# Four orders of the long and short passes in the up projection of a gated hybrid block

## The chip, the cores and the metric

The kernel runs on one core of one Trainium2 chip. The metric is the device time of the whole program in microseconds (us), the median of several runs. The kernel before took 1475.83 us (3 runs, 1475.67 to 1475.99).

## What is computed

The reference is one block on a sequence of 256 rows of 2048 features: an RMS norm, an input projection, three kinds of attention, a gated merge with an output projection, and a feed-forward part. The change lies in the feed-forward part alone:

```
h2 = rms_norm(x, g_ffn[l])
u = causal_depthwise_conv(h2 @ w_up[l], conv_w[l], conv_b[l])
u_gate, u_val = jnp.split(u, 2, axis=-1)
x = x + (jax.nn.silu(u_gate) * u_val) @ w_down[l]
```

`w_up` is 2048 x 11264 (twice D_FF = 5632), all in float32. The change is in the product `h2 @ w_up`.

## The kernel before, in words

A float32 product is made of passes in a rounded type (fp32r). Each operand is split into a high part and the low rest: the high part is the operand rounded to fp32r, the low part is what the rounding left. High by high, low by high and high by low are summed in PSUM, in float32.

**The stages.** In order of time they are the memory's keys and values, the input projection with the three attentions (line tags mq, f, s, g), the gated merge (g, b), the output projection (o), the up projection (u) with its convolution, and the down projection (d). Products other than u run through `passes` (lines 148 to 154) or `three` (lines 284 to 288) with three matmuls of up to 512 columns, each with a weight load of its own.

**The up stage.** The tile hT holds h2 transposed: for each of the 16 k tiles (128 features each, KT = 16) 512 columns, 256 of the high part and then 256 of the low part. The stage walks over 11 blocks of four feature tiles (f0 = 0, 4, ..., 40) and in each over the two halves of w_up (s = 0 for the gate, s = 1 for the value). One f0 with one s is called a *round* here; there are 22. A round fills four PSUM banks, ps[0] to ps[3], one for each tile of 128 features. It takes eight pieces of w_up of 128 x 1024 (two k tiles by 512 features). `piece` (lines 135 to 146) loads a piece by a DMA on SyncE's queue into raw, ScalarE casts it into hi (line 141), and VectorE subtracts to get lo (line 142). There are four buffers each of raw, hi and lo.

For each k tile and each of the four feature tiles there are two matmuls, with w_up as the stationary operand:
- the **long pass** (line 1152): weights hi, moving all 512 columns of hT(k), so it gives high by high and high by low at once, into the whole bank;
- the **short pass** (line 1153): weights lo, moving only the first 256 columns (the high part), added to the first half of the same bank.

So a k tile is eight matmuls, a round 128, and the stage 1408 long and 1408 short ones, each with a load of 128 x 128 weights (LDWEIGHTS). Before, they stand as long 0, short 0, long 1, short 1 and so on: always alternating, with the two passes of one feature tile side by side.

**What stands around them.** After each piece, `tick()` moves pending generators on by a step, at most two at a time: the convolutions of the round before (`conv`, from line 1113, which copy the upper half of a bank out at line 1118, add the lower half at 1120, scale, apply three taps and a bias, and for s = 1 form the product that goes into aT), and in the background sums of w_down that the down stage uses later (`weight_sums`). In the first rounds some transposes of the last parts of hT (line 195) stand between the passes. No order is pinned by hand for the matmuls of this stage; the framework schedules them in the order in which the code issues them, and places the other engines' work beside them.

Of the kernel before, what the change touches and what calls it, by code (L numbers as in the profile page):

```python
# [16 lines left out]
S = 256  # L17
# [18 lines left out]
BLOCKS = 14  # L36
WINDOW = 2
GS = 3


@with_exitstack
def hybrid_block(
# [25 lines left out]
    nc = tc.nc  # L68
# [12 lines left out]
    def bank(name):  # L81
        return pp.tile([P, 512], F32, tag="bank", name=name)
# [14 lines left out]
    def later(gen):  # L97
        waiting.append(gen)
# [3 lines left out]
    def tick(beside=True):  # L102
        if beside:
            for g in background:
                next(g, None)
        while waiting and len(active) < WINDOW:
            active.append([waiting.popleft(), 0])
        for a in list(active):
            if a[1] > 0:
                a[1] -= 1  # L110
                continue
            try:
                a[1] = next(a[0]) or 0
            except StopIteration:
                active.remove(a)
# [19 lines left out]
    def piece(src, a, n, name):  # L135
        raw = wp.tile([P, PIECE], F32, tag="raw", name=f"raw_{name}")
        hi = wp.tile([P, PIECE], F32R, tag="hi", bufs=SBUFS, name=f"hi_{name}")
        lo = wp.tile([P, PIECE], F32R, tag="lo", bufs=SBUFS, name=f"lo_{name}")
        m = a * n
        pin(nc.sync.dma_start(raw[:, :m].rearrange("p (a n) -> p a n", a=a), src))  # L140
        pin(nc.scalar.copy(hi[:, :m], raw[:, :m]))  # L141
        pin(nc.vector.tensor_tensor(lo[:, :m], raw[:, :m], hi[:, :m].bitcast(F32), ALU.subtract))  # L142
        return (
            hi[:, :m].rearrange("p (a n) -> p a n", a=a),
            lo[:, :m].rearrange("p (a n) -> p a n", a=a),
        )
# [9 lines left out]
    def product(x_of, w, nk, n0, n, name):  # L156

        ps = [bank(f"{name}_{t}") for t in range(NT)]
        wv = w.rearrange("(k p) n -> p k n", p=P)
        for k in range(0, nk, 2):  # L160
            a = min(2, nk - k)
            wh, wl = piece(wv[:, k : k + a, n0 : n0 + n], a, n, f"{name}_{k}")
            order = [(j, t) for j in range(a) for t in range(NT)]
            if k + a == nk:
                order.sort(key=lambda jt: jt[1])
            for j, t in order:
                xk = x_of(k + j)
                xs_ = xk[:, t * P : (t + 1) * P], xk[:, S + t * P : S + (t + 1) * P]
                three(ps[t][:, :n], *xs_, (wh[:, j], wl[:, j]), k + j == 0, k + j == nk - 1)
            tick()  # L170
        return ps
# [30 lines left out]
    def k_tiles(name):  # L202

        most = xt_pool.tile([P, KT - 2, 2 * S], F32R, tag="xt", name=name)
        rest = []

        def at(k):
            if k < KT - 2:
                return most[:, k]
            if not rest:  # L210
                rest.append(xt_pool.tile([P, 2, 2 * S], F32R, tag="xu", name=f"{name}_rest"))
            return rest[0][:, k - KT + 2]

        at.pair = lambda p: most[:, 2 * p : 2 * p + 2]
        return at
# [74 lines left out]
    def pair_sums(pair, w, groups):  # L290

        v = pair.bitcast(F32).rearrange("p k (l c) -> p k l c", l=2)
        a, r = (half.rearrange("p (i q) -> p i q", i=4) for half in (w[:, :512], w[:, 512:]))
        nc.vector.tensor_tensor(w[:, :512].rearrange("p (k c) -> p k c", k=2), v[:, :, 0], v[:, :, 1], ALU.add)

        a10 = a[:, 1:2].to_broadcast([P, 2, P])
        nc.vector.tensor_tensor(r[:, FS3 : FS1 + 1], a[:, 0:4:3], a10, ALU.subtract)
        nc.vector.scalar_tensor_tensor(r[:, FS2], r[:, FS1], -1.0, a[:, 0], ALU.mult, ALU.subtract)
        nc.vector.tensor_tensor(r[:, FS4], r[:, FS2], a[:, 2], ALU.add)
        for dst, which in groups:  # L300
            nc.scalar.copy(dst[..., 0, :], r[:, which])
        for dst, which in groups:
            nc.vector.tensor_tensor(dst[..., 1, :], r[:, which], dst[..., 0, :].bitcast(F32), ALU.subtract)
# [261 lines left out]
    def block(name, dt=F32):  # L565
        return bp.tile([P, 1024], dt, tag="blk", name=name)
# [105 lines left out]
    for k in range(KT):  # L672
# [18 lines left out]
        for _ in range(0 if k < 3 else 1 if k < 8 else 3):  # L691
            if squares:
                j, t = squares.popleft()
# [36 lines left out]
    ps = proj(C_MQ, MEM_W, "mq")  # L730
# [36 lines left out]
    for c in range(3):  # L767
        ps = proj(c * 512, 512, f"f{c}")
# [7 lines left out]
    ps = proj(1536, 512, "f3")  # L776
# [3 lines left out]
    ps = proj(2048, 262, "f4")  # L780
# [58 lines left out]

    xs = cst.tile([P, GS, 4, 2, P], F32R, tag="xres", name="xs")  # L840

    def x_sums():
        for p in range(GS):
            pair_sums(xT.pair(p), block(f"xw_{p}"), [(xs[:, p], slice(0, 4))])
            yield 2
# [9 lines left out]
    for c in range(3):  # L855
        ps = proj(C_SB + c * 512, 512, f"s{c}")
# [51 lines left out]
    ps = proj(C_SB + 1536, 512, "s3")  # L908
# [4 lines left out]
    ps = proj(C_SB + 2048, 256, "s4")  # L913
# [39 lines left out]
    for m in range(2):  # L953
        gate = []
        for b, plan in enumerate(g_plans[m]):
# [40 lines left out]
            if not plan:  # L996
                biases()
                for n in range(2):
                    ps = proj(c0 + n * 512, 512, f"g{n}_{b}")
# [12 lines left out]
        for n in range(2):  # L1012
            acc = gate[branches[0][3]][n]
            for i, (w, k0, nk, b) in enumerate(branches):
                ps = product(lambda k: oT[:, k0 + k], w[0], nk, (2 * m + n) * 512, 512, f"b{2 * m + n}_{b}")
# [15 lines left out]
    hT = k_tiles("hT")  # L1031
# [34 lines left out]
    for nb, plan in enumerate(o_plans):  # L1066
# [4 lines left out]
        for n in range(2):  # L1071
            for t in range(NT):
                o = xres[:, t, nb * PIECE + n * 512 : nb * PIECE + (n + 1) * 512]
# [12 lines left out]
    for i in range(2):  # L1086
        background.append(
            weight_sums(
                lambda name, i=i: ff.tile([P, 1024], F32, tag=f"end{i}", bufs=1, name=name), 8, 6, delay=14 + 2 * i
# [23 lines left out]
    def conv(ps, f, s):  # L1113
        if not pads:
            padded()
        ct = s * FT + f
        cr = cp.tile([P, S], F32, tag="cr", bufs=2, name=f"cr_{f}_{s}")
        nc.scalar.copy(cr, ps[:, S:])
        u = pads[f % 2]
        nc.vector.tensor_tensor(cr, cr, ps[:, :S], ALU.add)  # L1120
        nc.vector.tensor_tensor(u[:, 2:], cr, rbc, ALU.mult)  # L1121
        y = cp.tile([P, S], F32, tag="y", bufs=6, name=f"y_{f}_{s}")
        tap = lambda j: taps[:, j, ct : ct + 1]
        nc.scalar.activation(y, u[:, 2:], AF.Identity, scale=tap(2), bias=tap(3))  # L1124
        nc.vector.scalar_tensor_tensor(y, u[:, 1 : S + 1], tap(1), y, ALU.mult, ALU.add)
        nc.vector.scalar_tensor_tensor(y, u[:, 0:S], tap(0), y, ALU.mult, ALU.add)
        if s == 0:
            nc.scalar.activation(y, y, AF.Silu)
            ys[f] = y
        else:  # L1130
            g = ys.pop(f)
            nc.vector.tensor_tensor(g, g, y, ALU.mult)
            split_to(a_pair(f // 2)[:, f % 2], g)
        return
        yield

    for f0 in range(0, FT, 4):
        if f0 == FA:
            assert not halves
            for g in background:  # L1140
                deque(g, 0)
            background.clear()
        for s in range(2):
            ps = [bank(f"u{f0 + i}_{s}") for i in range(4)]
            c0 = s * D_FF + f0 * P
            for k in range(0, KT, 2):
                hi, lo = piece(upv[:, k : k + 2, c0 : c0 + 512], 2, 512, f"u{f0}_{s}_{k}")
                for j in range(2):
                    first, last = k + j == 0, k + j == KT - 1
                    for i in range(4):  # L1150
                        c = slice(i * P, (i + 1) * P)
                        nc.tensor.matmul(ps[i], lhsT=hi[:, j, c], rhs=hT(k + j), start=first, stop=False)  # L1152
                        nc.tensor.matmul(  # L1153
                            ps[i][:, :S], lhsT=lo[:, j, c], rhs=hT(k + j)[:, :S], start=False, stop=last
                        )
                tick()
            for i in range(4):
                later(conv(ps[i], f0 + i, s))
# [41 lines left out]
    for nb, plan in enumerate(d_plans):  # L1200
# [5 lines left out]
        for t in range(NT):  # L1206
            for n in range(2):
                c = nb * PIECE + n * 512
                o = xres[:, t, c : c + 512]
                nc.vector.tensor_tensor(o, o, X[t][n], ALU.add)  # L1210
                if (nb, t, n) == (1, 1, 1):
                    nc.scalar.dma_start(ov[:, t, c : c + 256], o[:, :256])
                    c, o = c + 256, o[:, 256:]
# [35 lines left out]
```

## Time and profile before

| | |
|---|---|
| median of 3 runs | 1475.83 us |
| the profiled execution's own time | 1476.04 us |
| its span in the trace | 1474.3 us |
| TensorE busy | 1468.7 us, 7337 matmuls |
| VectorE busy | 1195.8 us (81%) |
| ScalarE busy | 840.3 us (57%) |
| GpSimd busy | 20.4 us (1%) |
| DMA | 369.42 MB, 251 GB/s on average |
| up stage | from 746.7 us to about 1245.8 us |

In the rows of groups, the columns are the line, the engine, the operation, the tiles written and read, the shape (partitions x elements), the count, the busy time in us and the mean duration of one in ns, and last the idle time of the engine just before them. In a time line each row begins with the start in us from the span's start and the duration in us. A matmul's recorded duration runs past the start of the next one, since matmuls are pipelined; the distance from start to start is what one of them takes of TensorE's time. In rows of windows, the columns are the stretch, its length, the busy time and count of each engine (PE, PEld, DVE, ACT, POOL), the granted TensorE clock, the DMA share and GB/s.

### The profile page before, as it was taken

To read this page: it belongs to the slowest core of one execution; us is meant where nothing else is said; L and a number is where in the kernel's file an instruction comes from. 1 tells how busy PE (TensorE), PEld (TensorE's weight loads), DVE (VectorE), ACT (ScalarE), POOL (GpSimd) and SP (SyncE) were. 2 spreads that over 40 slices of the span, in tenths; PEclk is the share of its full clock that TensorE was granted. 3 is DMA by queue.
4 is the path that set the end of the run, shared out by engine and by line. 5 is a ranking of instruction groups with operands and counts; after the bars stand their busy time and mean duration, and the time that the engine had idled before them with its cause. 6 is when DMAs were issued, how large, how long until landed. Compare 5 with 4: busy or idle time off the path is not lost.

```text
span 1474.3 us, 20665 instructions
## 1 busy us (share of the span) xinstructions
PE 1468.7 (100%) x7337; PEld 1239.0 (84%) x7337; DVE 1195.8 (81%) x1818; ACT 840.3 (57%) x1194; POOL 20.4 (1%) x46
## 2 busy tenths in 40 slices
PE   9999999999999999999999999999999999999998
PEld 7888888888888888888888888888888888888887
DVE  5777676777588899997788888888888877997877
ACT  6755454464364555546666656656556555674664
POOL 0000000021000000000000000000000000000000
PEclk9999999999999999999999999999999999999999
DMA  9686787687768576878768888888888866798796
GB/s 313 198 274 194 219 285 216 179 277 219 247 203 272 168 222 207 279 250 282 238 207 272 279 283 285 272 271 287 279 279 283 260 185 199 241 315 276 257 328 224
DMA packets 205526, 369.42 MB, mean 251 GB/s; under 512 B 13530, under 2 KB 82030, under 8 KB 205166
## 3 DMA queue, kind: packets, MB, share of 16 engines
q1 hardware_dynamic: 204094, 365.99, 77.7%
q10 hardware_dynamic: 1328, 2.11, 0.4%
q8 instruction: 57, 0.93, 0.2%
q14 instruction: 47, 0.39, 0.1%
HBM read 335.54 MB, written 32.51 MB: 250 GB/s over the span
## 4 chain that ended last, share of the span: by engine, by line
PE 98%; DMA 0%; DVE 0%; ACT 0%; SPq 0%; POOL 0%; issue 0%; POOLq 0%; DVEq 0%
PE u L1152 22%; PE u L1153 11%; PE xd L288 4%; PE xd L287 4%; PE xd L286 4%; PE xg L288 3%; PE xg L287 3%; PE xg L286 3%; PE f L288 2%; PE f L286 2%; PE f L287 2%; PE s L286 2%; PE s L288 2%; PE s L287 2%; PE g L286 2%; PE g L288 2%
## 5 line engine op out<-in xcount | busy, mean ns | idle before, releaser
L1152 PE MATMUL u<-hT,hi_u 128*128 128x512 f32 x1232 | 436.2, 399 | 0.0
L1153 PE MATMUL u<-hT,lo_u 128*128 128x256 f32 x1232 | 345.9, 281 | 0.0
L1152 PEld LDWEIGHTS u<-hT,hi_u 128*128 128x128 f32 x1232 | 231.5, 188 | 57.5
L142 DVE TENSOR_TENSOR lo_u<-raw_u,hi_u 128x1024 fp32r<-128x1024 f32 x176 | 215.0, 1222 | 71.1 <-ACT hi_u L141 69.0
L141 ACT CAST hi_u<-raw_u 128x1024 fp32r<-128x1024 f32 x176 | 184.7, 1050 | 150.5 <-PE u L1152 134.1
L1153 PEld LDWEIGHTS u<-hT,lo_u 128*128 128x128 f32 x1232 | 232.7, 189 | 0.0
L281 DVE TENSOR_TENSOR lo_d<-raw_d,hi_d 128x1024 fp32r<-128x1024 f32 x88 | 106.6, 1221 | 20.8 <-ACT hi_d L280 18.0
L280 ACT CAST hi_d<-raw_d 128x1024 fp32r<-128x1024 f32 x88 | 91.8, 1053 | 48.1 <-PE xd L287 22.3
L280 ACT CAST hi_g<-raw_g 128x1024 fp32r<-128x1024 f32 (+1 forms) x64 | 61.7, 972 | 38.4 <-PE xg L287 10.2
L281 DVE TENSOR_TENSOR lo_g<-raw_g,hi_g 128x1024 fp32r<-128x1024 f32 (+1 forms) x64 | 70.9, 1117 | 4.3 <-ACT hi_g L280 4.3
L141 ACT CAST hi_f<-raw_f 128x1024 fp32r<-128x1024 f32 (+1 forms) x40 | 38.6, 967 | 52.0 <-PE f L287 47.3
L142 DVE TENSOR_TENSOR lo_f<-raw_f,hi_f 128x1024 fp32r<-128x1024 f32 (+1 forms) x40 | 44.7, 1119 | 27.9 <-ACT hi_f L141 26.0
L286 PE MATMUL xd<-hi_d,aT 128*128 128x512 f32 x170 | 66.2, 389 | 0.0
L287 PE MATMUL xd<-hi_d,aT 128*128 128x512 f32 x170 | 66.2, 389 | 0.0
L288 PE MATMUL xd<-lo_d,aT 128*128 128x512 f32 x170 | 66.2, 389 | 0.0
L142 DVE TENSOR_TENSOR lo_s<-raw_s,hi_s 128x1024 fp32r<-128x1024 f32 (+1 forms) x40 | 44.7, 1116 | 24.3 <-ACT hi_s L141 23.4
L141 ACT CAST hi_s<-raw_s 128x1024 fp32r<-128x1024 f32 (+1 forms) x40 | 38.4, 961 | 43.9 <-PE s L287 28.3
L1152 PE MATMUL u<-hT_rest,hi_u 128*128 128x512 f32 x176 | 63.1, 398 | 0.0
L141 ACT CAST hi_b<-raw_b 128x1024 fp32r<-128x1024 f32 x32 | 33.7, 1053 | 43.2 <-PE b L287 21.5
L142 DVE TENSOR_TENSOR lo_g<-raw_g,hi_g 128x1024 fp32r<-128x1024 f32 x32 | 39.3, 1232 | 22.7 <-ACT hi_g L141 22.3
L1124 ACT ACTIVATE y<-u,taps 128x256 f32<-128x256 f32 x88 | 49.2, 595 | 13.0 <-DVE u L1121 13.0
L141 ACT CAST hi_g<-raw_g 128x1024 fp32r<-128x1024 f32 x32 | 33.6, 1051 | 37.4 <-PE g L287 35.1
(481 smaller groups left out, 3531.9 us busy)
## 6 DMA issues: line engine op xcount, KB each, us to landing
raw_u<-in_w_up_dram SPq DMA_DIRECT2D x176, 512.0 KB, 4.9
raw_g<-in_w_in_dram SPq DMA_DIRECT2D x96, 512.0 KB, 4.3
raw_d<-in_w_down_dram SPq DMA_DIRECT2D x66, 512.0 KB, 5.5
pre_d<-in_w_down_dram SPq DMA_DIRECT2D x88, 256.0 KB, 4.6
kept_d<-pre_d SPq DMA_DIRECT2D x44, 512.0 KB, 6.3
raw_f<-in_w_in_dram SPq DMA_DIRECT2D x32, 512.0 KB, 4.8
raw_s<-in_w_in_dram SPq DMA_DIRECT2D x32, 512.0 KB, 3.9
raw_o<-in_w_out_dram SPq DMA_DIRECT2D x25, 512.0 KB, 5.6
```

The lines of the kernel that those rows point to most:

```text
L141: pin(nc.scalar.copy(hi[:, :m], raw[:, :m]))
L142: pin(nc.vector.tensor_tensor(lo[:, :m], raw[:, :m], hi[:, :m].bitcast(F32), ALU.subtract))
L280: nc.scalar.copy(hi[:, :n], src)
L281: nc.vector.tensor_tensor(lo[:, :n], src, hi[:, :n].bitcast(F32), ALU.subtract)
L286: fix(nc.tensor.matmul(o, lhsT=ah, rhs=w[0], start=first, stop=False))
L287: fix(nc.tensor.matmul(o, lhsT=al, rhs=w[0], start=False, stop=False))
L288: fix(nc.tensor.matmul(o, lhsT=ah, rhs=w[1], start=False, stop=last))
L1124: nc.scalar.activation(y, u[:, 2:], AF.Identity, scale=tap(2), bias=tap(3))
L1152: nc.tensor.matmul(ps[i], lhsT=hi[:, j, c], rhs=hT(k + j), start=first, stop=False)
L1153: nc.tensor.matmul(ps[i][:, :S], lhsT=lo[:, j, c], rhs=hT(k + j)[:, :S], start=False, stop=last)
```

## The change

The eight passes of a k tile are taken in one of four orders, and the orders change from round to round. In the strings, h is a long pass, l a short one, and the digit is the feature tile. Every bank still gets its long pass ahead of its short one in each k tile. The matmuls themselves, their operands and their number stay.

```diff
+UP_ORDERS = [
+    [(int(o[i + 1]), o[i]) for i in range(0, 16, 2)]
+    for o in ("h0l0h1l1h2l2h3l3", "h0h1l0h2l1h3l2l3", "h0h1l0l1h2h3l2l3", "h0h1h2h3l0l1l2l3")
+]
...
                 for j in range(2):
                     first, last = k + j == 0, k + j == KT - 1
-                    for i in range(4):
+                    for i, part in UP_ORDERS[(f0 // 2 + s) % len(UP_ORDERS)]:
                         c = slice(i * P, (i + 1) * P)
-                        nc.tensor.matmul(ps[i], lhsT=hi[:, j, c], rhs=hT(k + j), start=first, stop=False)
-                        nc.tensor.matmul(
-                            ps[i][:, :S], lhsT=lo[:, j, c], rhs=hT(k + j)[:, :S], start=False, stop=last
-                        )
+                        if part == "h":
+                            nc.tensor.matmul(ps[i], lhsT=hi[:, j, c], rhs=hT(k + j), start=first, stop=False)
+                        else:
+                            nc.tensor.matmul(
+                                ps[i][:, :S], lhsT=lo[:, j, c], rhs=hT(k + j)[:, :S], start=False, stop=last
+                            )
```

The orders are counted from 0. Blocks with f0 = 0, 8, 16, 24, 32, 40 take order 0 for the gate and order 1 for the value; blocks with f0 = 4, 12, 20, 28, 36 take orders 2 and 3. In the changed kernel the long pass is line 1157, the short one line 1159, and other lines below the table stand four or more further down.

TensorE, the round f0 = 4, s = 0 (order 2), the first k tile of its second piece, before. The names are the bank, hT, and the piece's hi or lo:

```order
L1152 MATMUL u_0_7183<-hT,hi_u_0_2_7239 128x512
L1153 MATMUL u_0_7183<-hT,lo_u_0_2_7240 128x256
L1152 MATMUL u_0_7184<-hT,hi_u_0_2_7239 128x512
L1153 MATMUL u_0_7184<-hT,lo_u_0_2_7240 128x256
L1152 MATMUL u_0_7185<-hT,hi_u_0_2_7239 128x512
L1153 MATMUL u_0_7185<-hT,lo_u_0_2_7240 128x256
L1152 MATMUL u_0_7186<-hT,hi_u_0_2_7239 128x512
L1153 MATMUL u_0_7186<-hT,lo_u_0_2_7240 128x256
```

The same k tile in the changed kernel:

```order
L1157 MATMUL u_0_7183<-hT,hi_u_0_2_7239 128x512
L1157 MATMUL u_0_7184<-hT,hi_u_0_2_7239 128x512
L1159 MATMUL u_0_7183<-hT,lo_u_0_2_7240 128x256
L1159 MATMUL u_0_7184<-hT,lo_u_0_2_7240 128x256
L1157 MATMUL u_0_7185<-hT,hi_u_0_2_7239 128x512
L1157 MATMUL u_0_7186<-hT,hi_u_0_2_7239 128x512
L1159 MATMUL u_0_7185<-hT,lo_u_0_2_7240 128x256
L1159 MATMUL u_0_7186<-hT,lo_u_0_2_7240 128x256
```

Two successions of long behind long and two of short behind short have come in where all had alternated.

TensorE, the next round (f0 = 4, s = 1, order 3) at the same place, in the changed kernel (before, it alternates like the piece above):

```order
L1157 MATMUL u_1_7422<-hT,hi_u_1_2_7474 128x512
L1157 MATMUL u_1_7423<-hT,hi_u_1_2_7474 128x512
L1157 MATMUL u_1_7424<-hT,hi_u_1_2_7474 128x512
L1157 MATMUL u_1_7425<-hT,hi_u_1_2_7474 128x512
L1159 MATMUL u_1_7422<-hT,lo_u_1_2_7475 128x256
L1159 MATMUL u_1_7423<-hT,lo_u_1_2_7475 128x256
L1159 MATMUL u_1_7424<-hT,lo_u_1_2_7475 128x256
L1159 MATMUL u_1_7425<-hT,lo_u_1_2_7475 128x256
```

All four long passes now stand ahead of the four short ones.

VectorE, in the round after that one (f0 = 8, s = 0, order 0), before. lo_u_0_4 and lo_u_0_6 are the splits of the third and fourth piece, cr and u the convolution's tiles:

```order
L142 TENSOR_TENSOR lo_u_0_4_7754<-raw_u_0_4_7752,hi_u_0_4_7753 128x1024
L1120 TENSOR_TENSOR cr_1_7686<-cr_1_7686,u_1_7422 128x256
L1120 TENSOR_TENSOR cr_1_7697<-cr_1_7697,u_1_7423 128x256
L1121 TENSOR_TENSOR u_6983<-cr_1_7686,rbc 128x256
L1121 TENSOR_TENSOR u_6985<-cr_1_7697,rbc 128x256
L142 TENSOR_TENSOR lo_u_0_6_7776<-raw_u_0_6_7774,hi_u_0_6_7775 128x1024
```

And in the changed kernel:

```order
L146 TENSOR_TENSOR lo_u_0_4_7754<-raw_u_0_4_7752,hi_u_0_4_7753 128x1024
L146 TENSOR_TENSOR lo_u_0_6_7776<-raw_u_0_6_7774,hi_u_0_6_7775 128x1024
L1124 TENSOR_TENSOR cr_1_7686<-cr_1_7686,u_1_7422 128x256
L1124 TENSOR_TENSOR cr_1_7697<-cr_1_7697,u_1_7423 128x256
L1125 TENSOR_TENSOR u_6983<-cr_1_7686,rbc 128x256
L1125 TENSOR_TENSOR u_6985<-cr_1_7697,rbc 128x256
L146 TENSOR_TENSOR lo_u_0_8_7798<-raw_u_0_8_7796,hi_u_0_8_7797 128x1024
```

The split of the fourth piece has moved ahead of the convolution's first four steps, and the later splits of the round have moved up likewise. SyncE's and GpSimd's rows stand as before.

## The prediction

> **What bounds the kernel now.** I read the page first: the span, its engine rows and its costliest groups. It is one execution on one core.
>
> ```profile
> span 1474.3 us, 20665 instructions
> PE 1468.7 (100%) x7337; PEld 1239.0 (84%) x7337; DVE 1195.8 (81%) x1818; ACT 840.3 (57%) x1194; POOL 20.4 (1%) x46
> L1152 PE MATMUL u<-hT,hi_u 128*128 128x512 f32 x1232 | 436.2, 399 | 0.0
> L1153 PE MATMUL u<-hT,lo_u 128*128 128x256 f32 x1232 | 345.9, 281 | 0.0
> L142 DVE TENSOR_TENSOR lo_u<-raw_u,hi_u 128x1024 fp32r<-128x1024 f32 x176 | 215.0, 1222 | 71.1 <-ACT hi_u L141 69.0
> ```
>
> TensorE is busy all the time, and the two lines that the change reorders never waited (0.0 in the last column; the fifth row is the split that makes lo). The durations of 399 and 281 ns are no price: matmuls are pipelined and these overlap. What an order can change is the distance from one matmul's start to the next, and the time line has the starts. Next come the whole stage by the windows, and what stands around line L1152 and around the casts that feed it:
>
> ```profile
> 746.00:1246.00 500.00, 500.00 (x2839) 434.01 (x2838) 420.58 (x723) 294.55 (x452) 0.00 (x0) 1.00 0.82 261
> ```
>
> ```profile
> L1152 PEld LDWEIGHTS u<-hT,hi_u x1232: 187/188/190, 746.5 to 1242.5; 128*128 128x128 f32 x176
> L1152 PE MATMUL u<-hT,hi_u x1232: 389/398/476, 746.7 to 1242.6; 128*128 128x512 f32 x176
> L1152 PE MATMUL u<-hT_rest,hi_u x176: 392/398/403, 768.0 to 1245.5; 128*128 128x512 f32 x176
> ```
>
> ```profile
>   PE u L1152: 134.1, 112
> ```
>
> The stage lasts 500 us; TensorE is busy in all of it at a granted clock of 1.00, VectorE in 420.58, ScalarE in 294.55, and DMA takes a 0.82 share. The last row is from the casts' own waits (line L141): ScalarE sat idle 134.1 us, 112 times, until a long pass had freed a buffer of hi. The producers are ahead of TensorE. So the stage is 1408 long and 1408 short passes back to back: from the first long pass at 746.7 to the last at 1245.5 there are 1407 pairs in 498.8 us, 354.5 ns each, with a few transposes among them. A short pass and a long one make a pair.
>
> **What one pair costs.** This is the time line of TensorE in the present order, three pairs:
>
> ```profile
> 905.22 0.40 PE L1152 MATMUL u<-hT_rest,hi_u 128*128 128x512 f32 x1
> 905.45 0.28 PE L1153 MATMUL u<-hT_rest,lo_u 128*128 128x256 f32 x1
> 905.57 0.40 PE L1152 MATMUL u<-hT_rest,hi_u 128*128 128x512 f32 x1
> 905.81 0.28 PE L1153 MATMUL u<-hT_rest,lo_u 128*128 128x256 f32 x1
> 905.93 0.40 PE L1152 MATMUL u<-hT_rest,hi_u 128*128 128x512 f32 x1
> 906.17 0.28 PE L1153 MATMUL u<-hT_rest,lo_u 128*128 128x256 f32 x1
> 906.28 0.40 PE L1152 MATMUL u<-hT_rest,hi_u 128*128 128x512 f32 x1
> ```
>
> From 905.22 to 906.28 are 1.06 us for three pairs: **353 ns a pair**, about 236 from a long pass to the short one and 117 back. The three are not equal (0.35, 0.36, 0.35); this cycle repeats through the stage. The new orders put long behind long and short behind short, which the stage does not have. Other stages do, each matmul with weights of its own as here: long ones in the down stage, then passes of 256 columns (line tags s, 300 to 307 us; the rows left out are seven more of the same).
>
> ```profile
> 1299.65 0.39 PE L286 MATMUL xd<-hi_d,aT 128*128 128x512 f32 x1
> 1299.87 0.39 PE L287 MATMUL xd<-hi_d,aT 128*128 128x512 f32 x1
> 1300.10 0.39 PE L288 MATMUL xd<-lo_d,aT 128*128 128x512 f32 x1
> 1300.33 0.39 PE L286 MATMUL xd<-hi_d,aT 128*128 128x512 f32 x1
> ```
>
> ```profile
> 302.81 0.28 PE L286 MATMUL s<-hi_s,xT 128*128 128x256 f32 x1
> ...
> 303.77 0.28 PE L288 MATMUL s<-lo_s,xT 128*128 128x256 f32 x1
> ```
>
> Three steps of 0.68 us in all give 227 ns for long behind long; eight steps of 0.96 us give 120 for short behind short. Together 347: **6 ns less than the present pair**. That alternation need not cost the 6 ns shows in this stage itself. After the transposes at 752 us the same alternating order runs for 16 us in another cycle; the first and last long pass of 20 pairs there:
>
> ```profile
> 761.03 0.39 PE L1152 MATMUL u<-hT,hi_u 128*128 128x512 f32 x1
> ...
> 767.97 0.39 PE L1152 MATMUL u<-hT_rest,hi_u 128*128 128x512 f32 x1
> ```
>
> 6.94 us by 20 is 347 ns. So TensorE has a settled pace of 347 per pair and a worse cycle of 353, and before is in the worse one nearly throughout. Which one it falls into hangs on what preceded, by a few ns.
>
> **The change, part by part.** Nothing is added or taken away: 1408 long and 1408 short passes, the same loads, the same DMAs. SyncE's and GpSimd's order is untouched.
> - Rounds. The index is (f0/2 + s) mod 4 with f0 in steps of 4: even blocks take orders 0 and 1, odd blocks 2 and 3. Eleven blocks give 6, 6, 5 and 5 rounds. Order 0 is the present one. In order 1 one of eight successions in a k tile is long-long and one short-short, in order 2 two and two, in order 3 three and three; the rest alternate, the seam between k tiles included (each order ends short and begins long). A round has 16 k tiles, so 16 x (6x1 + 5x2 + 5x3) = 496 times a long-short and a short-long succession are replaced by a long-long and a short-short.
> - Price of one replacement: 227 + 120 - 353 = -6 ns (-6.6 with the three pairs taken as 353.3 and the three steps as 226.7). 496 x 6.6 = **3.3 us less**, if the successions that still alternate stay at 353.
> - VectorE and ScalarE. After an order-3 round the list puts some splits one place earlier, ahead of the convolution's taps. They cost nothing while TensorE waits for neither: VectorE has 500 - 420.58 = 79 us free in the stage, and a stage 3.3 us shorter leaves 76. If that cover were gone, one split late would hold TensorE by at most its own length, which the row of line L142 gives as 1222 ns; I take zero, since not one wait of TensorE for it is on record there.
> - Buffers. In order 3 the last long pass on a hi tile comes three short passes (0.36 us) earlier, so casts may start earlier; lo is first needed later in the k tile. Both only loosen. New accumulators are asked for together at a round's start in order 3; each bank was filled two rounds (some 45 us) before, and its copying out is queued behind that round's end, so zero here as well.
>
> What no row shows is a succession such as long-long-short-short repeating. From below: every pair of the 16 changed rounds at 347, that is 16 x 64 = 1024 pairs x 6.6 = 6.8 us less. If the order-0 rounds that follow a changed round come into the good cycle as well (5 x 64 pairs), another 2.1. From above: the longs behind the last short of the stage:
>
> ```profile
> 1245.71 0.28 PE L1153 MATMUL u<-hT_rest,lo_u 128*128 128x256 f32 x1
> 1245.83 0.40 PE L286 MATMUL xd<-hi_d,aT 128*128 128x512 f32 x1
> ...
> 1246.78 0.39 PE L287 MATMUL xd<-hi_d,aT 128*128 128x512 f32 x1
> ```
>
> The row at 1246.78 is the fourth long behind the first: 0.95 us for four, 237 each, 11 above the settled 227, so a long pass is slower for a while after short ones. Four such longs and four shorts at 120 make a k tile of 1.427 us against 4 x 0.3533 = 1.413: +14 ns. In all 256 changed k tiles that is 3.5 us more. The opposite seam is milder: behind passes of 262 columns three longs take 0.69 us, 230 each.
>
> ```profile
> 192.45 0.40 PE L286 MATMUL s<-hi_s,xT 128*128 128x512 f32 x1
> ...
> 193.14 0.40 PE L286 MATMUL s<-hi_s,xT 128*128 128x512 f32 x1
> ```
>
> And the first shorts behind longs are not dearer than 120: three steps take 0.35 us.
>
> ```profile
> 293.81 0.28 PE L286 MATMUL s<-hi_s,xT 128*128 128x256 f32 x1
> ...
> 294.16 0.28 PE L286 MATMUL s<-hi_s,xT 128*128 128x256 f32 x1
> ```
>
> With four longs at 230 and four shorts at 118 a k tile takes 1.39 us, 21 ns less; I lean to this side and take the 3.3 us, nearer to the middle of the ends than to either.
>
> **The sum.** The profiled execution took 1476.04 us (span 1474.3 and 1.7 around it). Less 3.3 is 1472.7. The median of the runs shown, 1475.83, lies 0.2 lower, so I predict **1472.5 us**.
>
> **The rivals.**
> - *All settles.* The changed rounds find the 347 pace throughout: 1475.83 - 6.8 = 1469.0, down to 1467 with the order-0 rounds. For it: 347 is what all settled rows give, in this stage too. Against: the present order leaves that pace and stays at 353 for hundreds of us.
> - *Order does not matter.* Each pass costs the same wherever it stands, 353 a pair being this stage's own price (its tiles, its banks, the traffic beside it): 1475.8, give or take 1. For it: TensorE's clock is already 1.00 and nothing waits. Against: 347 at 761 us, with the same tiles. The Trainium skill, in "TensorE: Matmul & The Clock Gate", section "Back-to-back issue gap", gives 518 cycles for 512 columns and 262 for 256, whatever the neighbour; at its 2.4 GHz I estimate 325 ns a pair from that page in any order, hence no change. The trace does not agree with the figure (353), and by the two cycles not with the independence either.
> - *Shorts unsettle the longs behind them* (slower). The 237 ns at 1246 us is paid in every run of longs, as no run of longs is longer than four: +3.5 us, 1479.3. It decides once a changed pair is above 353.3; above 356.2 (2.95 us by 1024 pairs) it would show as slower by 0.2%. For it: that seam comes out of this very order. Against: the 230 at 192 us.
> - A short pass too brief to cover a load of weights would be worse (the load's record is 188 ns), but in the rows at 303 us every short pass has such a load and they stand 120 apart; I leave it no chance of its own.
>
> **How the numbers follow.** My forecast 36 in 100, with a range of its own from 1471 to 1474.3; all settles 21; order does not matter 18; shorts unsettle 25. 0.2% is 2.95 us, about what a measurement of this kernel can tell from no change: below 1472.88 is faster. The forecast is cut in two by it, 18 and 18; all settles is faster; the third is within; of the slower case 15 are beyond 1478.78 and 10 within. So faster 0.39, same 0.46, slower 0.15. The range 1468.0 to 1479.3 takes the bounds of both unknown sides; left out are the good cycle in order-0 rounds too, and a slower case beyond its price.
>
> **What would show it.** In the time line of the changed kernel: pairs of order 0 at 353 or 347; in orders 1 to 3 a k tile of eight passes between 1.387 and 1.427 us, order 3 below order 2 below order 1 if my count of replacements is right; about equal at 1.387 if all settles; 1.413 in every order if order does not matter; long-long steps near 237 if shorts unsettle. TensorE must keep 0.0 idle on both lines. A wait on hi, lo or a bank there, or a k tile outside those bounds, makes the prediction wrong in its premise, not in its size.

## The result, and the profile after

The changed kernel takes 1471.12 us (median of 10 runs, 1470.69 to 1473.0), the kernel before 1475.91 us beside it: a ratio of 0.9969, 95% interval 0.9959 to 0.9979, or 4.8 us less. One of the ten executions of the kernel before took 2846.36 us and is not in the ratio; its other nine lie between 1475.46 and 1477.38. The profiled span went from 1474.3 to 1469.3 us. The page of the changed kernel, its span, TensorE's row and its two lines:

```profile
span 1469.3 us, 20673 instructions
PE 1464.2 (100%) x7337; PEld 1238.8 (84%) x7337; DVE 1192.3 (81%) x1818; ACT 837.7 (57%) x1194; POOL 20.3 (1%) x46
L1157 PE MATMUL u<-hT,hi_u 128*128 128x512 f32 x1232 | 393.5, 395 | 0.0
L1159 PE MATMUL u<-hT,lo_u 128*128 128x256 f32 x1232 | 274.2, 280 | 0.0
```

As many matmuls as before, and 0.0 of waiting on both lines. The casts still wait for TensorE to free a buffer, 121.0 us in 96 waits, as the waits of line L145 (before, L141) show:

```profile
  PE u L1157: 121.0, 96
```

So the stage is bound as it was, and TensorE itself goes through the same matmuls faster. Where, the starts of the rounds tell. These are the first long passes of the second to the seventh round in the time line of the changed kernel:

```profile
770.65 0.48 PE L1157 MATMUL u<-hT,hi_u 128*128 128x512 f32 x1
...
793.32 0.40 PE L1157 MATMUL u<-hT,hi_u 128*128 128x512 f32 x1
...
815.62 0.40 PE L1157 MATMUL u<-hT,hi_u 128*128 128x512 f32 x1
...
838.05 0.40 PE L1157 MATMUL u<-hT,hi_u 128*128 128x512 f32 x1
...
860.25 0.39 PE L1157 MATMUL u<-hT,hi_u 128*128 128x512 f32 x1
...
882.84 0.40 PE L1157 MATMUL u<-hT,hi_u 128*128 128x512 f32 x1
```

The distances are 22.67 us for the round of order 1, 22.30 for order 2, 22.43 for order 3, **22.20 for order 0**, and 22.59 for order 1 again. This sequence repeats to the end of the stage (22.59, 22.30, 22.44, 22.19 us by the trace's nanoseconds). Before, a round took 22.61 us, except the first of all, which has the transposes in it, and the second (22.69). The stage has become 4.7 us shorter:

| order | rounds that changed | us a round, before and after | us in all |
|---|---|---|---|
| 0 | 5 (behind order 3) | 22.61, 22.19 | 2.1 |
| 1 | 6 | 22.61, 22.59 (the first: 22.69, 22.67) | 0.1 |
| 2 | 5 | 22.61, 22.30 | 1.6 |
| 3 | 5 | 22.61, 22.44 | 0.9 |

The largest part came in the rounds in which **no matmul has moved**. There the passes alternate at the good pace, which before showed for some 16 us only; first and last long pass of 20 pairs in the changed kernel:

```profile
849.85 0.39 PE L1157 MATMUL u<-hT,hi_u 128*128 128x512 f32 x1
...
856.78 0.39 PE L1157 MATMUL u<-hT,hi_u 128*128 128x512 f32 x1
```

6.93 us by 20 is 347 ns. In the kernel before, the pace changes at two places, and at both transposes stand between the passes, whose own order stays the same. At the first the stage comes into the good pace, across 16 transposes:

```profile
749.88 0.40 PE L1152 MATMUL u<-hT,hi_u 128*128 128x512 f32 x1
...
752.00 0.40 PE L1152 MATMUL u<-hT,hi_u 128*128 128x512 f32 x1
...
752.35 1.91 PE L195 MATMUL hT<-ident,xres_again 128*128 128x128 f32 x16
...
754.79 0.39 PE L1152 MATMUL u<-hT,hi_u 128*128 128x512 f32 x1
...
756.18 0.39 PE L1152 MATMUL u<-hT,hi_u 128*128 128x512 f32 x1
```

Six pairs take 2.12 us ahead of them, 353 ns each, and four take 1.39 behind, some 347 each. At the second, between the first and the second round, it falls out of it across two:

```profile
770.74 0.38 PE L1048 MATMUL rp<-ident,rb 128*128 128x128 f32 x2
770.88 0.48 PE L1152 MATMUL u<-hT,hi_u 128*128 128x512 f32 x1
771.19 0.28 PE L1153 MATMUL u<-hT,lo_u 128*128 128x256 f32 x1
771.31 0.40 PE L1152 MATMUL u<-hT,hi_u 128*128 128x512 f32 x1
...
773.43 0.40 PE L1152 MATMUL u<-hT,hi_u 128*128 128x512 f32 x1
```

From 771.31 on six pairs take 2.12 us again. The first long pass behind the two transposes holds TensorE for 0.31 us, which is why the second round took 22.69. No run here leaves these two transposes out.

In a k tile of order 1 (in the time line, equal neighbours are one row with their count, so x2 are two passes):

```profile
875.77 0.63 PE L1157 MATMUL u<-hT,hi_u 128*128 128x512 f32 x2
876.24 0.28 PE L1159 MATMUL u<-hT,lo_u 128*128 128x256 f32 x1
876.35 0.40 PE L1157 MATMUL u<-hT,hi_u 128*128 128x512 f32 x1
876.59 0.28 PE L1159 MATMUL u<-hT,lo_u 128*128 128x256 f32 x1
876.70 0.40 PE L1157 MATMUL u<-hT,hi_u 128*128 128x512 f32 x1
876.94 0.40 PE L1159 MATMUL u<-hT,lo_u 128*128 128x256 f32 x2
877.18 0.63 PE L1157 MATMUL u<-hT,hi_u 128*128 128x512 f32 x2
```

The tile runs from 875.77 to 877.18, 1.41 us, no shorter than the old order's (4 x 0.3533 = 1.413). Its two longs together take 0.47 us, where settled ones took 0.454. Order 2, eight passes from the middle of one k tile to the middle of the next, and the start of the following half:

```profile
894.69 0.63 PE L1157 MATMUL u<-hT,hi_u 128*128 128x512 f32 x2
895.15 0.39 PE L1159 MATMUL u<-hT,lo_u 128*128 128x256 f32 x2
895.38 0.63 PE L1157 MATMUL u<-hT,hi_u 128*128 128x512 f32 x2
895.85 0.40 PE L1159 MATMUL u<-hT,lo_u 128*128 128x256 f32 x2
896.08 0.63 PE L1157 MATMUL u<-hT,hi_u 128*128 128x512 f32 x2
```

1.39 us. The rows are rounded to 0.01 us and cannot tell the lengths of the two halves apart (697 and 696 ns from start to start by the trace's nanoseconds), but the halves are not alike inside: the row of shorts lasts 0.39 in the first and 0.40 in the second. In the first the starts of the two shorts and of the next long stand 117 and 112 ns apart, in the second 114 and 119. That small difference turns out to matter below.

### The profile page after: what moved, and what is told of

Its sections match the earlier page's. It is cut to its first block, busy times and chain, and to the rows that moved or that the text cites. A ratio compares the mean times of both kernels' runs of the same rounds, so it can differ in the third digit from the quotient of the medians.

```text
span 1469.3 us, 20673 instructions
## 1 busy us (share of the span) xinstructions
PE 1464.2 (100%) x7337; PEld 1238.8 (84%) x7337; DVE 1192.3 (81%) x1818; ACT 837.7 (57%) x1194; POOL 20.3 (1%) x46
## 4 chain that ended last, share of the span: by engine, by line
PE 99%; DVE 0%; ACT 0%; POOL 0%; issue 0%; POOLq 0%; DVEq 0%
PE u L1157 22%; PE u L1159 11%; PE xd L292 4%; PE xd L291 4%; PE xd L290 4%; PE xg L292 3%; PE xg L290 3%; PE xg L291 3%; PE f L290 2%; PE f L292 2%; PE f L291 2%; PE s L290 2%; PE s L292 2%; PE s L291 2%; PE g L290 2%; PE b L292 2%
## 5 line engine op out<-in xcount | busy, mean ns | idle before, releaser
L1157 PE MATMUL u<-hT,hi_u 128*128 128x512 f32 x1232 | 393.5, 395 | 0.0
L1159 PE MATMUL u<-hT,lo_u 128*128 128x256 f32 x1232 | 274.2, 280 | 0.0
L145 ACT CAST hi_u<-raw_u 128x1024 fp32r<-128x1024 f32 x176 | 184.9, 1051 | 151.8 <-PE u L1157 121.0
L1159 PEld LDWEIGHTS u<-hT,lo_u 128*128 128x128 f32 x1232 | 222.3, 188 | 26.7
L1157 PEld LDWEIGHTS u<-hT,hi_u 128*128 128x128 f32 x1232 | 210.8, 188 | 27.6
L285 DVE TENSOR_TENSOR lo_d<-raw_d,hi_d 128x1024 fp32r<-128x1024 f32 x88 | 106.7, 1222 | 20.6 <-ACT hi_d L284 17.6
L145 ACT CAST hi_f<-raw_f 128x1024 fp32r<-128x1024 f32 (+1 forms) x40 | 38.6, 967 | 52.2 <-PE f L291 47.3
L145 ACT CAST hi_s<-raw_s 128x1024 fp32r<-128x1024 f32 (+1 forms) x40 | 38.4, 961 | 43.9 <-PE s L291 27.4
L145 ACT CAST hi_b<-raw_b 128x1024 fp32r<-128x1024 f32 x32 | 33.5, 1051 | 41.7 <-PE b L291 18.7
L1157 PE MATMUL u<-hT_rest,hi_u 128*128 128x512 f32 x176 | 56.4, 395 | 0.0
L145 ACT CAST hi_g<-raw_g 128x1024 fp32r<-128x1024 f32 x32 | 33.6, 1051 | 38.3 <-PE g L291 34.7
```

Of the source, the lines that this page charges most:

```text
L285: nc.vector.tensor_tensor(lo[:, :n], src, hi[:, :n].bitcast(F32), ALU.subtract)
L1159: nc.tensor.matmul(ps[i][:, :S], lhsT=lo[:, j, c], rhs=hT(k + j)[:, :S], start=False, stop=last)
```

## Experiments

Two explanations stood against each other at first. The *count theory* is the prediction's own sum: each long-long with a short-short in place of two alternating successions saves 6.6 ns, and what still alternates stays as it was. The *path theory*: for a given order TensorE falls into one of several lasting cycles, and what preceded decides which. The order-0 rounds of the changed kernel speak for the second; the runs were to say whether that lasts and what decides. Edits are against the changed kernel; they replace the index of the table, unless the text says otherwise. In them f0 // 2 + s is the round and k + j the k tile, both counted from 0. Ratios are to the kernel before.

**Order 3 in one round.**

```diff
-for i, part in UP_ORDERS[(f0 // 2 + s) % len(UP_ORDERS)]:
+for i, part in UP_ORDERS[3 if f0 // 2 + s == 1 else 0]:
```

> Order 3 in the second round alone (f0 = 0, s = 1), order 0 in the other 21. Path theory (the pace of alternating passes hangs on what preceded it, and lasts): the 20 rounds behind it take 22.19 us each, as the order-0 rounds behind order 3 did in the changed kernel, against 22.61 before: 20 x 0.42 = 8.4 us less, and 0.2 in the second round, so about 1467.3 us. Count theory (each long-long and short-short in place of two alternating successions saves 6.6 ns, order-0 rounds stay at 22.61): 48 replacements, 0.3 us less, 1475.6 us. If the good pace lasts for one round only: 0.6 us less, 1475.3.

1475.87 us, ratio 1.0000 (0.9991 to 1.0009). The order-0 rounds behind it take 22.61 us each. The path theory's forecast failed in its simple form: order 3 ahead is not enough. The count theory's 1475.6 is met here within the noise.

**Order 3 in one k tile.**

```diff
+for i, part in UP_ORDERS[3 if (f0 // 2 + s, k + j) == (1, 4) else 0]:
```

> Order 3 in a single k tile (the fifth of the second round), order 0 everywhere else: eight matmuls in another order out of 2816. Path theory: if one run of four longs and four shorts is enough to change the cycle, all that follows runs at 22.19 us a round, 20.7 rounds x 0.42 = 8.7 us less, 1467.2 us; if it takes more than one such tile, 1475.9. Count theory: three replacements, 0.02 us, 1475.9.

1476.19 us, ratio 1.0003 (0.9994 to 1.0012). The tile itself took 1.388 us, the next one 1.411, and all behind it stayed in the worse cycle.

**A tour of the orders.**

```diff
+for i, part in UP_ORDERS[int("0100200300100200301000"[f0 // 2 + s])]:
```

> Orders by round 0 1 0 0 2 0 0 3 0 0 1 0 0 2 0 0 3 0 1 0 0 0: order 0 behind each of the others, for up to three rounds, and each of the others behind good and behind bad rounds. Path theory: order-0 rounds come in two prices, 22.19 and 22.61 us, set by the order that stood last before them (behind order 3: 22.19), the rounds of one group all alike. Count theory: every order-0 round at 22.61, order 1 at 22.50, order 2 at 22.40, order 3 at 22.29, and 208 replacements x 6.6 = 1.4 us less in all, 1474.5.

A single execution: 1468.55 us, span 1466.8. The reading rests on the rounds in its trace. All of the 14 order-0 rounds behind the second round take 22.19 us, whether behind order 1, 2 or 3, and for up to three rounds on end; order 1 is at 22.59, order 2 at 22.29, order 3 at 22.44. The count theory's rounds (22.50, 22.40, 22.29, and 22.61 for order 0) are off in each line and its total by 6 us: it falls. But order 3 leaves order 0 good here and bad in the first experiment, so the order ahead does not decide alone.

**Order 2 throughout.**

```diff
+for i, part in UP_ORDERS[2]:
```

> Order 2 (long long short short) in all 22 rounds. Path theory: it settles in the cycle it had in the changed kernel, 22.30 us a round against 22.61, so 21 x 0.31 = 6.5 us less, 1469.4 us, if it does not need order 1 ahead of it; otherwise anything from 22.19 to 22.6 a round. Count theory: 22 x 32 = 704 replacements x 6.6 = 4.6 us less, 1471.3.

1468.99 us, ratio 0.9956 (0.9943 to 0.9970); 22.29 us in each round from the third on. So order 2 has one pace and keeps it; it took the same behind order 1 in the changed kernel (22.30) and behind order 0 in the tour (22.29).

**Order 2 in one round.**

```diff
+for i, part in UP_ORDERS[2 if f0 // 2 + s == 1 else 0]:
```

> Order 2 in the second round alone, order 0 in the other 21. Path theory, as the tour left it (order 0 behind order 2 came out at 22.19 us a round, and stayed there): 22.37 us for the second round and 22.19 for the 20 behind it, 0.3 + 20 x 0.42 = 8.7 us less than before, 1467.1 us. Count theory: 32 replacements, 0.2 us, 1475.6. If the good cycle cannot last over many rounds: between the two, with a round in which the pace changes back in the trace.

1475.42 us, ratio 0.9995 (0.9987 to 1.0004): a miss. The round itself took 22.38 us, and the 20 behind it 22.61 each.

The two misses with a whole round have one thing in common in the trace. Order 3 has a cycle of two k tiles (1.400 and 1.406 us), order 2 one of the two kinds of half tile seen above. In these two misses the round ended on a tile of 1.406 us, and on a half tile whose shorts last 0.40; ahead of good order-0 rounds it ended on a tile of 1.400, and on a half tile whose shorts last 0.39. That is a *phase*, and it can be turned by leaving out the last tile, or half tile.

**Order 3 for 15 tiles, and order 2 for 15 and a half.**

```diff
+for i, part in UP_ORDERS[3 if f0 // 2 + s == 1 and k + j < 15 else 0]:
```

The second of them, with a fifth order in the table:

```diff
-    for o in ("h0l0h1l1h2l2h3l3", "h0h1l0h2l1h3l2l3", "h0h1l0l1h2h3l2l3", "h0h1h2h3l0l1l2l3")
+    for o in ("h0l0h1l1h2l2h3l3", "h0h1l0h2l1h3l2l3", "h0h1l0l1h2h3l2l3", "h0h1h2h3l0l1l2l3", "h0h1l0l1h2l2h3l3")
...
+for i, part in UP_ORDERS[(2 if k + j < 15 else 4) if f0 // 2 + s == 1 else 0]:
```

> As the kernel with order 3 in the whole second round (which left order 0 at 22.61), but the 16th k tile of that round in order 0: one tile less. In order 3 the tiles alternate 1.400 and 1.406 us, and the order-0 rounds were good behind a tile of the one kind (changed kernel, tour) and bad behind one of the other. Path theory with this two-tile phase: good from there on, 0.2 + 20 x 0.42 = 8.6 us less, 1467.2 us. If the phase of the tiles has nothing to do with it: bad as with 16 tiles, 1475.9.

> As the kernel with order 2 in the whole second round (which left order 0 in the worse cycle: its last short pass ended a half tile whose shorts stand 113 and 119 ns ahead of the next), but the second half of the round's last k tile in order 0, so that order 2 ends on a half tile of the other kind (116 and 112 ns), as it did ahead of the good rounds in the tour. Path theory with a phase of half tiles: good from there on, 22.38 us and then 20 rounds of 22.19, 0.3 + 20 x 0.42 = 8.7 us less than before, 1467.2 us. If the order alone counted, with its place in the program: as with the whole round, 1475.6.

1467.12 us, ratio 0.9940 (0.9925 to 0.9955), and 1467.19 us, ratio 0.9942 (0.9927 to 0.9956). Both as the phase said, within 0.1 us. The seam with all 16 tiles of order 3: the last tile, and 22 pairs of order 0 behind it.

```profile
793.26 1.09 PE L1157 MATMUL u<-hT_rest,hi_u 128*128 128x512 f32 x4
794.19 0.64 PE L1159 MATMUL u<-hT_rest,lo_u 128*128 128x256 f32 x4
794.66 0.40 PE L1157 MATMUL u<-hT,hi_u 128*128 128x512 f32 x1
...
802.43 0.40 PE L1157 MATMUL u<-hT,hi_u 128*128 128x512 f32 x1
```

And with 15 tiles, the same number of pairs:

```profile
790.93 1.09 PE L1157 MATMUL u<-hT_rest,hi_u 128*128 128x512 f32 x4
791.86 0.63 PE L1159 MATMUL u<-hT_rest,lo_u 128*128 128x256 f32 x4
792.33 0.40 PE L1157 MATMUL u<-hT_rest,hi_u 128*128 128x512 f32 x1
...
799.97 0.39 PE L1157 MATMUL u<-hT,hi_u 128*128 128x512 f32 x1
```

7.77 us against 7.64 for 22 pairs of the same code: 353 and 347 ns. Ahead of the seam the two differ in the last row of shorts, 0.64 and 0.63 us. The end of order 2 in the round with all 16 tiles:

```profile
792.00 0.63 PE L1157 MATMUL u<-hT_rest,hi_u 128*128 128x512 f32 x2
792.47 0.40 PE L1159 MATMUL u<-hT_rest,lo_u 128*128 128x256 f32 x2
792.70 0.40 PE L1157 MATMUL u<-hT,hi_u 128*128 128x512 f32 x1
```

And with fifteen and a half:

```profile
791.57 0.63 PE L1157 MATMUL u<-hT_rest,hi_u 128*128 128x512 f32 x2
792.03 0.39 PE L1159 MATMUL u<-hT_rest,lo_u 128*128 128x256 f32 x2
792.26 0.40 PE L1157 MATMUL u<-hT_rest,hi_u 128*128 128x512 f32 x1
```

The rounds behind take 22.61 us in the first case and 22.19 in the second.

**Order 1 for three tiles.**

```diff
+for i, part in UP_ORDERS[1 if f0 // 2 + s == 1 and k + j < 3 else 0]:
```

> Order 1 in the first three k tiles of the second round alone, order 0 everywhere else: 24 matmuls in another order. In the tour order 1 left order 0 in the good cycle each of three times, from one k tile on behind it. Path theory: three tiles are enough to reach its own steady cycle (there, the third tile already took 1.413 us as all later ones), and good from then on: about 0.35 us less in the second round and 20 x 0.42 behind it, 8.7 us less, 1467.1 us. Count theory: nothing, 1475.9.

1466.47 us, ratio 0.9938 (0.9921 to 0.9954), the fastest here that computes the same sums as the kernel before: three k tiles, 24 matmuls out of 2816, are in another order. The first long pass of the third round and of the last one:

```profile
792.76 0.40 PE L1157 MATMUL u<-hT,hi_u 128*128 128x512 f32 x1
...
1214.30 0.40 PE L1157 MATMUL u<-hT,hi_u 128*128 128x512 f32 x1
```

421.54 us for 19 rounds, 22.19 each: the good cycle, once entered, holds to the end of the stage. No transposes stand among the passes there.

**Neighbours in other banks.** Two orders only, the second one new:

```diff
-    for o in ("h0l0h1l1h2l2h3l3", "h0h1l0h2l1h3l2l3", "h0h1l0l1h2h3l2l3", "h0h1h2h3l0l1l2l3")
+    for o in ("h0l0h1l1h2l2h3l3", "h0l2h1l3h2l0h3l1")
...
+for i, part in UP_ORDERS[0 if k + j in (0, KT - 1) else 1]:
```

> Still alternating long and short, in k tiles 2 to 15 of every round, but the short pass goes to a bank two further on (h0 l2 h1 l3 h2 l0 h3 l1), so that no two neighbours write the same bank; first and last k tile in order 0. Path theory (only lengths count, the bank does not): as before, good in the first round and 22.61 us in the others, 1475.9 us. If the worse cycle comes from a short pass that follows a long one into the same bank: 14 of 16 tiles at 1.387, 21 x 0.36 = 7.6 us less, 1468.2.

1476.05 us, ratio 1.0002 (0.9993 to 1.0011), 22.61 us a round. In 14 of the 16 k tiles no short pass follows a long one into its own bank, and the worse cycle runs on all the same: the bank is not what keeps it up.

**Other lengths of the short pass.** Order 0 everywhere, `:S` replaced in the short pass's output and its hT operand, by the first line in one kernel and by the second in another:

```diff
+ps[i][:, : S + 8], lhsT=lo[:, j, c], rhs=hT(k + j)[:, : S + 8], start=False, stop=last
...
+ps[i][:, : S - 8], lhsT=lo[:, j, c], rhs=hT(k + j)[:, : S - 8], start=False, stop=last
```

> Order 0 everywhere, the short pass 264 columns wide instead of 256 (low part times low part is added for 8 columns, which the kernel before leaves out). Eight columns more cost 3.3 ns at the rate at which 256 more columns cost 107 ns (227 against 120). If the pace is the columns plus a fixed price: each pair 3.3 ns more, 1408 x 3.3 = 4.7 us, 1480.5 us. Path theory (the pair locks in a cycle that hangs on the lengths): no such sum; the pair may be anything from 350 (which would be less than the 353.3 of the narrower pass, and 4.3 us faster than 1475.8) to 360 ns (9 us slower).

> Order 0 everywhere, the short pass 248 columns wide: low weights by high part is left out for 8 of 256 columns. The settled price as the runs left it (columns at 2.4 per ns and 13.3 ns for each matmul) gives 343.3 ns a pair; the pass of 264 columns kept it (350.0). If 256 is bad alone because both its lengths lie on one grid, 248 settles at 343.3: 21 rounds x 64 x 10 = 13.4 us less, and 0.2 in the first round, 1462.2 us. If 248 has a worse cycle too, of 350 ns as 256 has 353.3: 4.6 us less, 1471.3. With only columns taken off the present cycle: 350.0 as well.

With 264 columns 1471.27 us, ratio 0.9969 (0.9958 to 0.9980): **more work in less time**. First and last long pass of 21 pairs:

```profile
899.64 0.40 PE L1157 MATMUL u<-hT,hi_u 128*128 128x512 f32 x1
...
906.99 0.39 PE L1157 MATMUL u<-hT,hi_u 128*128 128x512 f32 x1
```

7.35 us, 350.0 ns a pair. With 248 columns, which leaves out low by high for eight of the 256, 1462.36 us, ratio 0.9914 (0.9900 to 0.9929); 20 pairs:

```profile
899.67 0.39 PE L1157 MATMUL u<-hT,hi_u 128*128 128x512 f32 x1
...
906.54 0.39 PE L1157 MATMUL u<-hT,hi_u 128*128 128x512 f32 x1
```

6.87 us, 343.5 ns; by whole rounds (21.97 us for 64 pairs) 343.3. With 346.7 for 256 in the good cycle the three lie on a line of 3.3 ns for eight columns; the 353.3 of before lies 6.7 above it.

**264 columns in one round.** Order 0 everywhere:

```diff
+w = S + 8 if f0 // 2 + s == 1 else S
+ps[i][:, :w], lhsT=lo[:, j, c], rhs=hT(k + j)[:, :w], start=False, stop=last
```

> Order 0 everywhere, no pass moved; the short pass 264 columns wide in the second round alone, 256 in the others. It asks whether the order of passes is needed at all to leave the worse cycle, or any shift of some ns is enough. Path theory: the second round 22.48 us as in the kernel with 264 columns everywhere, and the 20 behind it all at 22.19 (1467.2 us) or all at 22.61 (1475.6 us), by the phase in which the last wide pass ends; both are open ahead of the run, and nothing between them. Count theory, and any theory in which the order itself is cheaper: 1475.6 us, no other result possible.

1475.38 us, ratio 0.9999 (0.9989 to 1.0009); the round took 22.48 us, those behind it 22.61. The path theory had both outcomes open, so this run decides nothing: whether one round of wider passes can lead into the good cycle stays open. That no change in the order of the passes is needed shows in the trace of the kernel before, where the pace became good across 16 transposes at 752 us.

## Why the prediction was right, and where its working was wrong

- *TensorE sets the stage, and nothing else comes in.* Right. No wait on either line, the same loads, and the splits that the schedule moved on VectorE cost nothing. All of the stage's 4.7 us are in the distances between starts.
- *There is a settled pace of 347 ns and a worse cycle of 353, and what preceded decides.* Right, and it is the cause of the largest part, the 2.1 us of the order-0 rounds; the other 2.6 are the paces that orders 2 and 3 have of their own. It came from the 20 pairs at 761 us, the row that carried most in the prediction.
- *Price of one replacement, -6.6 ns.* Wrong as a price. By the count, order 1 should save 0.11 us a round, order 2 0.21, order 3 0.32; they saved 0.02, 0.31 and 0.17. The neighbours in a run of one or two do not have the prices of a long stream, 227 and 120: in order 1 two longs take 0.47 us, not 0.454. The prediction's own test, order 3 below order 2 below order 1, failed: a k tile took 1.403 us in order 3 on average, 1.393 in order 2 and 1.413 in order 1.
- *"If the successions that still alternate stay at 353."* This is the step that failed. In the five order-0 rounds behind a changed round they went to 347 and gave 2.1 us, just the amount worked out for that case, which the prediction had put outside its forecast. 3.3 was forecast, 4.8 measured; the orders 1 to 3 by themselves gave 2.6. That the total came out near was in part luck: the 2.1 made up for the 0.7 that the orders fell short, and more. Whether those rounds get the good pace hangs on the phase at the seam, for which the prediction had no term; with order 3 in the second round alone they stayed at 353.
- *The slower rival* (shorts unsettle the longs behind them) is right about the longs: they keep above 230 ns in order 1 and in order 2 too (two take 0.46 to 0.47 us). Its time did not come, as shorts became cheaper as well (in order 2 two take 0.23 us, not 0.24), and every changed order was at least as fast as the old one.
- *Order does not matter* is refuted by the tour: one sequence of matmuls stood at 353 and at 347 ns a pair. The "whatever the neighbour" beside it was the prediction's own reading: the Trainium skill, in "TensorE: Matmul & The Clock Gate", section "Back-to-back issue gap", gives its 518 and 262 cycles for an isolated matmul. At its 2.4 GHz I estimate 216 and 109 ns from them; the long streams of this case took 226.7 and 120.

Shown by the runs: the cycles, that they last, that the phase at the seam selects them (turned as forecast in two pairs of kernels), that the bank does not keep the worse one up, and that 248 and 264 columns do not have the worse one in these runs. Not shown: what makes the phase. The weight loads are one candidate, since the record of each is 187 to 190 ns long and begins 2 to 5 ns behind the start of a matmul in the traces, but no run took them away.

## What to carry to other kernels

When the bounding engine never waits, compare the distance from start to start with the same instructions elsewhere in the trace; a pair that costs more than its two settled prices (here 353 against 227 and 120) can be a sign of a cycle that can be left. Look for a stretch in which the very same code runs faster, since it shows the attainable pace without any model, and at what stands where its pace changes (here a few transposes). A few instructions in another order (here 24 of 2816, 1466.47 us) can be worth more than reordering everything (order 2 throughout, 1468.99), and an operand eight columns wider as much as the whole change (a ratio of 0.9969 each). A gain of that kind has to be checked by stretches of the trace, because the total does not tell which of them gave it.

## What the runs showed of the hardware that was not expected

- The same alternating passes of 512 and 256 columns run at 346.7 or 353.3 ns a pair for hundreds of us (421.54 us in the kernel with three tiles of order 1), by how they were entered. In the kernel before, the good pace began behind 16 transposes at 752 us and ended at two at 770.74 us.
- The settled prices lie on one line. In long streams 512 columns take 226.7 ns and 256 take 120, so 256 columns more cost 106.7 ns, which is 2.4 columns per ns, and 13.3 ns are left for each matmul. By this line pairs of 512 with 248, 256 and 264 columns take 343.3, 346.7 and 350.0 ns, and that is what was measured.
- 264 columns are faster than 256 in the worse cycle: 350.0 against 353.3 ns a pair, 1471.27 against 1476.10 us.
